# Rows of decays spread to 128 partitions by DMAs of the GpSimd queue instead of products with one-hot columns

## The chip, the core and the metric

The kernel runs on one core of one Trainium2 chip. The core has five instruction streams that run beside each other and meet only at semaphores: TensorE (PE, the matrix engine), VectorE (DVE), ScalarE (ACT), GpSimd (POOL) and SyncE (SP). Each takes its instructions strictly in order, so one that waits holds up all behind it on its engine. Data come in by DMAs, which SP and POOL issue here. The metric is the device time of one execution in microseconds (us), as the median of several runs.

## What is computed

A trunk of two layers over one sequence of 512 tokens, 1024 features, in float32. Each layer is

```
x += 1/2 SwiGLU(RMSNorm(x))
x += W_out concat[mLSTM | retention | gated DeltaNet](RMSNorm(x))
x += 1/2 SwiGLU(RMSNorm(x))
```

and a last RMSNorm follows. The change is in the middle step, the mixer. Two of its three parts weigh pairs of tokens by decays that come from a running quantity per head and token:

```
# gated DeltaNet, per head, per chunk
g = cumsum(log_alpha);  decay[i, j] = exp(g[i] - g[j])   where j <= i
a_mat = I + strict(kb k^T * decay);  sol = triangular_solve(a_mat, rhs)
qk = (q k^T) * decay;  o = (q * exp(g)) S + qk u
# mLSTM, per head, per chunk
w[i, j] = exp(bcum[i] - bcum[j] + i_pre[j] - m_row[i])   where j <= i
```

Both need, for every head, a row of 512 numbers (g, or a running maximum) that varies along the free dimension and is the same on all 128 partitions, while the other index of the pair lies on the partitions. There are 8 such rows in a layer: 4 for the heads of mLSTM, 4 for those of DeltaNet.

## The kernel before, in words

Activations lie with features on the partitions and the 512 tokens along the free dimension. A float32 product is made of three fast products: each weight tile and each activation is split in a high part (`wh`, `xh`) and a low part (`wl`, `xl`), and `mm3` adds wh*xh, wh*xl and wl*xh in one bank of PSUM. The feed-forward steps save some of these products by a scheme of sums (tiles `px`, `py`, `pz`); `pd` are their down projections.

The mixer (`mixer`, from line 793) computes 32 tiles of the input projection (`pin` with features on the partitions, `ptok` with tokens there), 24 fast products each, and 8 tiles of the output projection (`po`). Between these dense products PE gets the small ones of the three recurrences. Each recurrence is written as generators (`gate_math`, `decays`, `delta_inverse`, `q_post`, `chain`, `mlstm`, `retention` and others), which sit in 12 lanes. A planner (`Clock`, `poll`) keeps a guessed time for each engine while the program is recorded and decides after every three dense products which generators may record a step; `wait` holds a generator until a named mark is set. The order that comes out is then fixed in the program: at run time each engine goes through it and waits where a semaphore isn't there yet.

A weight tile of the mixer takes two DMAs of 512 KB. SP loads the raw tile (`wr`). For the low part ACT writes the negated rounded tile to `wl` (line 309), and POOL then issues a DMA that adds the same weights onto it from memory (line 310, `wl<-win`); ACT and DVE write `wh`. `weights` starts the split two tiles ahead. All POOL DMAs go through one queue, named q0 in the profile; those of SP are q1.

The rows of decays: `gate_math` transposes the running sums to 8 rows of 512 (`prow`, line 948), copies them to SBUF and makes the running maximum of the four mLSTM rows by a scan (lines 950 and 951). ACT writes the rounded rows to partitions 0 to 7 of `RB`, DVE the remainder to partitions 32 to 39, and the mark `rows` is set (lines 953 to 957). `SEL` holds one-hot columns, with ones at j and 32 + j. `bcast_row` (line 863) multiplies column j, repeated 128 times, with `RB`: one product of 128x512 on PE, whose result is row j on every partition of a PSUM bank. It is called in three places:

- `decays` (line 1049): four banks `pG`, from which DVE makes `X`, and ACT the exponentials in place; `delta_inverse` multiplies `L` with these.
- `mlstm` (line 1362), once for each of two pairs of heads: two banks `pM`, from which DVE makes the halves of `w1` and other things.
- `q_post`, once for each of four heads: a bank `pG`, from which DVE makes `PT` and ACT the factor `eG` (in a tile `m` or `cs`).

That is 12 products in a layer, 24 in all.

Of the kernel before, what the change touches and what calls it, by code (L numbers as in the profile page):

```python
# [9 lines left out]
F32 = mybir.dt.float32  # L10
F32R = mybir.dt.float32r
I32 = mybir.dt.int32
AF = mybir.ActivationFunctionType
ALU = mybir.AluOpType
AX = mybir.AxisListType

P = 128
S = 512
# [8 lines left out]
INV = 4  # L27
BACKLOG = 1.65
VFIRST = 0.3
WARM = 11  # L30
OUT_KEYS = [("s0",), ("s1",), ("s2",), ("s3",)] + 4 * [("s4", "s5", "s6", "s7")]
GATES = (0, 1, 4, 5, 6, 7, 2, 3)
# [15 lines left out]
    merge_pairs="V c V V c V".split(),  # L48
    mlstm="V A V A V A G V V Vc Vc".split(),
    norm_cols="V A".split(),  # L50
    q_post="A VA A VG".split(),
    retention="VG Vc c".split(),
    rope="VG cG VG cG VG cG VG c".split(),
    split_weights="A c c".split(),
# [7 lines left out]
O_GQ, O_GK, O_GV, O_GZ, O_GA = 2056, 2568, 3080, 3592, 4104  # L62


C_ID, C_TRI, C_ONE, C_MT, C_MS, C_M32, C_COS, C_SIN, C_HALF, C_SEL, C_DEC, C_QD, C_KD, C_GC, C_SUM, C_END = (
    0, 128, 256, 260, 388, 516, 580, 708, 836, 838, 846, 1358, 1614, 1618, 1620, 1636)


Q_N1, Q_NM, Q_N2, Q_MG, Q_RG, Q_GG, Q_CONV, Q_BIAS, Q_ALOG = 0, 8, 16, 24, 26, 28, 32, 80, 96
# [3 lines left out]
def const_table():  # L73
    c = np.zeros((P, C_END), np.float32)
    r = np.arange(P)
    c[:, C_ID:C_ID + P] = np.eye(P)
    c[:, C_TRI:C_TRI + P] = r[:, None] <= r[None, :]
    c[:, C_ONE] = 1.0
    c[:, C_MT:C_MT + P] = np.where(r[:, None] <= r[None, :], 0.0, NEG)
    c[:, C_MS:C_MS + P] = np.where(r[:, None] > r[None, :], 0.0, NEG)  # L80
    c[:, C_M32:C_M32 + 32] = r[:, None] // 32 % 2 == 0
    inv = np.float32(10000.0) ** (-np.arange(0, 64, 2, dtype=np.float32) / np.float32(64))
    ang = (np.arange(S, dtype=np.float32)[:, None] * inv[None, :].astype(np.float32)).astype(np.float64)
    for col, f in ((C_COS, np.cos), (C_SIN, np.sin)):
        c[:, col:col + P] = f(ang).astype(np.float32).reshape(NT, P, 32).transpose(1, 0, 2).reshape(P, P)
    c[:, C_HALF] = r % 2 == 0
    c[:, C_HALF + 1] = r % 2 == 1
    for j in range(8):
        c[j, C_SEL + j] = c[32 + j, C_SEL + j] = 1.0

    lg = np.log1p(-np.exp2(-5.0 - np.arange(4)))
    rel = r[None, :] - r[:, None]
    for j, g in enumerate(lg):
        c[:, C_DEC + j * P:C_DEC + (j + 1) * P] = np.where(rel >= 0, np.exp(np.maximum(rel, 0) * g) * 0.125, 0.0)
        half = slice(64 * (j % 2), 64 * (j % 2) + 64)
        c[half, C_QD + (j // 2) * P:C_QD + (j // 2 + 1) * P] = np.exp((r + 1.0) * g)
        c[:, C_KD + j] = np.exp((P - 1.0 - r) * g) * 0.125
        c[half, C_GC + j // 2] = np.exp(P * g)
    c[:, C_SUM:C_SUM + 16] = r[:, None] % 32 == np.arange(16)[None, :]
    return c  # L100
# [67 lines left out]
def trunk(ctx, tc, a, out):  # L168
# [21 lines left out]
    T, V, A, G = Engine(nc.tensor, "T"), Engine(nc.vector, "V"), Engine(nc.scalar, "A"), Engine(nc.gpsimd, "G")  # L190

    cst = ctx.enter_context(tc.tile_pool(name="cst", bufs=1))
# [33 lines left out]
    def SM(s):  # L226
        if clk[0] is not None:
            clk[0].bank()
        return psm.tile([P, S], F32, name=nm(s), tag="sm")

    def r(ap):
        return ap.bitcast(F32R)
# [11 lines left out]
    def v3(ap, b):  # L244
        return ap.rearrange("p (a b) -> p a b", b=b)

    def bc(ap2, n):
        return ap2.unsqueeze(2).broadcast_to([ap2.shape[0], ap2.shape[1], n])


    C = cst.tile([P, C_END], F32, name="C")
# [3 lines left out]
    maskT = C[:, C_MT:C_MT + P]  # L255
    maskS = C[:, C_MS:C_MS + P]
    half = [C[:, C_HALF + i:C_HALF + i + 1] for i in (0, 1)]

    def bc4(m):
        return m.unsqueeze(1).broadcast_to([P, 4, P])  # L260
# [6 lines left out]

    h = cst.tile([P, KT, S], F32, name="h")
    Z4 = cst.tile([4, 1], F32, name="Z4")
    SEL = cst.tile([P, 8], F32, name="SEL")  # L270
    RB = cst.tile([P, S], F32, name="RB")
    zero = cst.tile([P, 1], F32, name="zero")


    plan, ends = [], deque()
# [492 lines left out]
    def mixer(l, n, nxt, after):  # L768
        q = prm[l]
        ck_ = clk[0] = Clock()  # L770
        marks = ck_.marks

        kdec, gl = COL("kdec", 16), COL("gl", 16)
# [6 lines left out]
        tm = [TMP("m", 520) for _ in range(8)]  # L780
# [79 lines left out]
        def wait(*keys):  # L860
            yield keys

        def bcast_row(ps, j):
            m = ps.shape[0]
            T.matmul(ps, r(SEL[:, j:j + 1].broadcast_to([P, m])), r(RB), start=True, stop=True)

        def norm_cols():
            n.stats()
# [5 lines left out]
        def gate_math():  # L874
# [71 lines left out]
            prow = SM("prow")  # L946
            for t in range(NT):
                T.transpose(prow[0:8, t * P:(t + 1) * P], ag3[:, t, :], ident)
            row = tm[6][0:8, 0:S]
            V.tensor_copy(row, prow[0:8, :])  # L950
            V.tensor_tensor_scan(row[0:4, :], Z4.broadcast_to([4, S]), prow[0:4, :], 0.0, ALU.add, ALU.max)
            yield
            A.copy(r(RB[0:8, :]), row)
            yield
            V.tensor_sub(r(RB[32:40, :]), row, RB[0:8, :])
            env.update(bg3=bg3, ag3=ag3, ng3=ng3, bt=bt)
            mark("rows")
            yield
# [88 lines left out]
        L, X, Tm = U("L"), U("X"), U("Tm")  # L1047

        def decays():

            yield from wait("rows")
            bg3 = env["bg3"]
            for hd in range(4):
                pG = SM("pG")
                bcast_row(pG, 4 + hd)
                E = X[:, hd, :]
                V.tensor_tensor(v3(E, P), bc4(maskS), v3(pG, P), ALU.subtract)
                V.tensor_copy(gl[:, hd * 4:hd * 4 + 4], v3(pG, P)[:, :, P - 1])
                yield
                for t in range(NT):  # L1060
                    s = slice(t * P, (t + 1) * P)
                    A.activation(E[:, s], E[:, s], AF.Exp, bias=bg3[:, t, 4 + hd:5 + hd])
                if hd == 3:
                    mark("decays")
                yield
            bght = bg3[:, :, 4:8].rearrange("p t h -> p h t")
            V.tensor_tensor(v3(kdec, 4), v3(gl, 4), bght, ALU.subtract)
            yield
            A.activation(kdec, kdec, AF.Exp)
            A.activation(eglast, gl, AF.Exp)  # L1070
            eg = COL("eg", 16)
            A.activation(v3(eg, 4), bght, AF.Exp)
            env["eg"] = eg
            mark("eg")
            yield
# [132 lines left out]
        def q_post(hd, kT, qT, odd):  # L1208
            yield from wait(f"q{hd}", "Um")
            if "PT" not in env:  # L1210
                env["PT"] = U("PT")
            PT = env["PT"]
            eG = scratch()[:, 2, :] if odd else tm[7][:, 0:S]
            bg3, ng3 = env["bg3"], env["ng3"]
            ps = to_tok(qT[:, hd, :])
            A.activation(PT[:, hd, :], ps, AF.Square)
            yield
            V.tensor_reduce(ssq[:, hd * 4:hd * 4 + 4], v3(PT[:, hd, :], P), AX.X, ALU.add)
            pG = SM("pG")
            bcast_row(pG, 4 + hd)  # L1220
            V.tensor_tensor(v3(PT[:, hd, :], P), v3(pG, P), bc4(maskT), ALU.add)
            A.activation(eG, pG, AF.Exp)
            yield
            for t in range(NT):
                s = slice(t * P, (t + 1) * P)
                A.activation(PT[:, hd, s], PT[:, hd, s], AF.Exp, bias=ng3[:, t, hd:hd + 1])
            yield
            pp = SM("pP")
            for t in range(NT):
                s = slice(t * P, (t + 1) * P)  # L1230
                T.matmul(pp[:, s], kT[:, hd, s], qT[:, hd, s], start=True, stop=True)
            V.tensor_tensor(PT[:, hd, :], pp, PT[:, hd, :], ALU.mult)
            G.tensor_tensor(qT[:, hd, :], qT[:, hd, :], eG, ALU.mult)
            mark(f"pq{hd}")
            yield
# [127 lines left out]
        def mlstm(pair, mqk, V1):  # L1363
            yield from wait("rows", "mqk", "vv")
            ag3 = env["ag3"]
            h0 = 2 * pair
            Es = [w1[:, 0:S], w1[:, S:2 * S]]
            kw, qs = w2[:, 0:384], w2[:, 384:768]
            mc, mp = COL("mc", 8), COL("mp", 4)
            for b in range(2):  # L1370
                pM = SM("pM")
                bcast_row(pM, h0 + b)
                V.tensor_tensor(v3(Es[b], P), bc4(maskT), v3(pM, P), ALU.subtract)
                hb = slice(64 * b, 64 * b + 64)
                V.tensor_copy(mc[:, 4 * b:4 * b + 4], v3(pM, P)[:, :, P - 1])
                V.tensor_copy(mp[hb, :], mc[hb, 4 * b:4 * b + 4])
                V.tensor_tensor(v3(qs[hb, :], P), bc(mp[hb, 0:3], P), v3(pM[hb, :], P)[:, 1:4, :], ALU.subtract)
                yield
                for t in range(NT):
                    c = slice(t * P, (t + 1) * P)  # L1380
                    A.activation(Es[b][:, c], Es[b][:, c], AF.Exp, bias=ag3[:, t, h0 + b:h0 + b + 1])
                yield
# [336 lines left out]
        T.matmul(warm, idle[:, 0:P], idle, start=True, stop=True)  # L1719
    n = Blocks(prm[0][:, Q_N1:Q_N1 + 8])  # L1720
    G.memset(Z4, 0.0)
    G.memset(zero, 0.0)
    sqs = {}

    def summed(d):
# [19 lines left out]
    summed(7)  # L1745
    gu.load_a(2)
    n.todo += [step for p in range(4) for step in n.sums(p)]
    n.todo.append(lambda: (A.copy(r(SEL), C[:, C_SEL:C_SEL + 8]), A.copy(r(RB), zero.broadcast_to([P, S]))))
    for l in range(DEPTH):
        nm_ = Norm(prm[l][:, Q_NM:Q_NM + 8])  # L1750
        ffn(n, stages[l][0], nm_)
# [73 lines left out]
```

## Time and profile before

| | |
|---|---|
| median of three runs | 2028.41 us (2026.38 to 2029.28) |
| the profiled execution's own time | 2026.25 us |
| its span, first to last instruction | 2024.5 us |
| PE busy | 1992.9 us, 98% |
| DVE busy | 1412.9 us, 70% |
| ACT busy | 1077.3 us, 53% |
| POOL busy | 268.9 us, 13% |
| granted TensorE clock, mean | 0.996 |
| moved by DMAs | 270.18 MB, 133 GB/s |

The profile is one execution. Busy time is what an engine spent in its instructions; matmuls overlap each other, so the time that one adds is read from the distance of two starts, not from its own length. The granted clock is a share of TensorE's upper level (1.00 is 2.4 GHz, 0.50 is 1.2 GHz). In the span the mixer of the first layer lies at about 365 to 620 us, that of the second at about 1360 to 1615.

### The profile page before, as it was taken

To read this page: it belongs to the slowest core of one execution; us is meant where nothing else is said; L and a number is where in the kernel's file an instruction comes from. 1 tells how busy PE (TensorE), PEld (TensorE's weight loads), DVE (VectorE), ACT (ScalarE), POOL (GpSimd) and SP (SyncE) were. 2 spreads that over 40 slices of the span, in tenths; PEclk is the share of its full clock that TensorE was granted. 3 is DMA by queue.
4 is the path that set the end of the run, shared out by engine and by line. 5 is a ranking of instruction groups with operands and counts; after the bars stand their busy time and mean duration, and the time that the engine had idled before them with its cause. 6 is when DMAs were issued, how large, how long until landed. Compare 5 with 4: busy or idle time off the path is not lost.

```text
span 2024.5 us, 32377 instructions
## 1 busy us (share of the span) xinstructions
PE 1992.9 (98%) x12865; PEld 1765.9 (87%) x12865; DVE 1412.9 (70%) x2447; ACT 1077.3 (53%) x1607; POOL 268.9 (13%) x311
## 2 busy tenths in 40 slices
PE   9999999999999999999999999999999999999997
PEld 6999988787888899998889998877878889999886
DVE  6888934568676788883588887335777758888623
ACT  5666622564476566662365555227545756655521
POOL 0000001134212100000010000013132120000000
PEclk9999999999999999999999999999999999999999
DMA  5555422664457466633256663237734655565231
GB/s 191 156 158 161 110 96 91 174 167 105 97 116 187 122 162 162 164 99 108 94 142 158 159 160 109 86 101 176 168 84 104 150 148 151 157 157 157 90 109 50
DMA packets 77928, 270.18 MB, mean 133 GB/s; under 512 B 8912, under 2 KB 11216, under 8 KB 77776
## 3 DMA queue, kind: packets, MB, share of 16 engines
q1 hardware_dynamic: 54080, 184.73, 25.6%
q0 software_dynamic: 22608, 82.32, 24.3%
q8 instruction: 101, 1.65, 0.3%
q10 hardware_dynamic: 1088, 1.05, 0.1%
q14 instruction: 51, 0.42, 0.1%
HBM read 265.97 MB, written 2.10 MB: 132 GB/s over the span
## 4 chain that ended last, share of the span: by engine, by line
PE 90%; DVE 5%; issue 2%; DMA 1%; ACT 1%; SPq 0%; POOL 0%; DVEq 0%; ACTq 0%; POOLq 0%
PE pd L182 22%; PE px L182 16%; PE pin L182 12%; PE pz L182 11%; PE py L182 11%; PE ptok L182 3%; PE pu L182 3%; PE pg L182 2%; DVE X L182 1%; PE pav L182 1%; DVE wl L182 1%; DMA wl<-win 1%; PE po L182 1%; PE ptr L182 1%; DMA m<-wgt 1%
## 5 line engine op out<-in xcount | busy, mean ns | idle before, releaser
L182 PE MATMUL pd<-hid,wh 128*128 128x512 f32 (+1 forms) x1320 | 403.9, 388 | 1.1 <-ACT wh L182 1.1
L182 ACT CAST wh<-wr 128x512 fp32r<-128x512 f32 (+2 forms) x392 | 308.3, 809 | 11.7 <-DMA wr<-w1gu 5.4
L182 DVE TENSOR_TENSOR wl<-wr,wh 128x1024 fp32r<-128x1024 f32 (+2 forms) x276 | 279.1, 1048 | 42.5 <-ACT wh L182 42.2
L182 PEld LDWEIGHTS pd<-hid,wh 128*128 128x128 f32 x1320 | 246.3, 189 | 55.2 <-ACT wh L182 1.3
L182 PE MATMUL pd<-hid,wl 128*128 128x512 f32 (+1 forms) x660 | 255.8, 388 | 0.8 <-DVE wl L182 0.8
L182 PE MATMUL px<-ub,wh 128*128 128x256 f32 x1264 | 232.6, 282 | 1.4 <-DVE g L182 1.4
L182 PE MATMUL py<-ub,wh 128*128 128x256 f32 x1264 | 229.2, 282 | 2.3 <-ACT wh L182 2.3
L182 ACT ACTIVATE g<-g 128x512 f32<-128x512 f32 x96 | 60.5, 632 | 283.7 <-DVE g L182 283.7
L182 DVE TENSOR_TENSOR wl<-s,wh 128x1024 fp32r<-128x1024 f32 x158 | 193.1, 1222 | 12.6 <-ACT wh L182 9.9
L182 PEld LDWEIGHTS py<-ub,wh 128*128 128x128 f32 x1264 | 194.3, 189 | 2.7 <-ACT wh L182 2.7
L182 PEld LDWEIGHTS px<-ub,wh 128*128 128x128 f32 x1264 | 193.8, 188 | 2.5 <-DVE g L182 2.2
L182 PE MATMUL py<-ub,wl 128*128 128x256 f32 x632 | 177.8, 281 | 1.5 <-DVE wl L182 1.5
L182 PE MATMUL pz<-xl,wh 128*128 128x256 f32 x632 | 178.1, 282 | 0.0
L182 ACT ACTIVATE xh<-h,prm 128x512 fp32r<-128x512 f32 x48 | 34.6, 722 | 269.4 <-DVE h L182 268.9
L182 PE MATMUL pz<-xh,wh 128*128 128x256 f32 x632 | 177.6, 281 | 0.0
L182 PE MATMUL px<-ub,wl 128*128 128x256 f32 x632 | 177.5, 281 | 0.0
L182 DVE SCALAR_TENSOR_TENSOR d<-pd,rb 128x512 f32<-128x512 f32 (+1 forms) x33 | 22.3, 675 | 222.3 <-PE pd L182 222.3
L182 PE MATMUL pz<-xh,wl 128*128 128x256 f32 x632 | 177.2, 280 | 0.0
L182 ACT CAST wh<-s 128x1024 fp32r<-128x1024 f32 x158 | 164.7, 1042 | 0.0
L182 PE MATMUL pin<-xh,wh 128*128 128x512 f32 x384 | 161.2, 420 | 0.0
L182 PE MATMUL pin<-xh,wl 128*128 128x512 f32 x384 | 151.3, 394 | 2.5 <-DMA wl<-win 2.5
L182 PE MATMUL pin<-xl,wh 128*128 128x512 f32 x384 | 151.2, 394 | 0.0
(602 smaller groups left out, 4363.4 us busy)
## 6 DMA issues: line engine op xcount, KB each, us to landing
wr<-w2gu SPq DMA_DIRECT2D x88, 512.0 KB, 5.7
wr<-w1gu SPq DMA_DIRECT2D x86, 512.0 KB, 5.6
wr<-win SPq DMA_DIRECT2D x64, 512.0 KB, 4.9
wl<-win POOLq DMA_DIRECT2D x62, 512.0 KB, 6.5
s<-w2gu POOLq DMA_DIRECT2D x40, 512.0 KB, 5.7
s<-w1gu POOLq DMA_DIRECT2D x39, 512.0 KB, 5.7
wr<-w1d SPq DMA_DIRECT2D x32, 512.0 KB, 4.4
wr<-w2d SPq DMA_DIRECT2D x32, 512.0 KB, 4.3
```

Source lines behind the costliest of these rows:

```text
L182: i = f(*a_, **k_)
```

## The change

`RB`, `SEL` and the products with them go, and so do the two steps in `gate_math` that filled `RB`. The 8 rows stay in a tile `ROWS` of 8 partitions. A new function issues a DMA of the POOL queue that reads one row of `ROWS` 128 times and writes it to the 128 partitions of an SBUF tile (256 KB written), and tells the planner that the row is there 3.0 us after its own time:

```diff
+LAND = 3.0
-        def bcast_row(ps, j):
-            m = ps.shape[0]
-            T.matmul(ps, r(SEL[:, j:j + 1].broadcast_to([P, m])), r(RB), start=True, stop=True)
+        def spread(dst, j, key):
+
+            G.dma_start(out=dst, in_=ROWS[j:j + 1, :].unsqueeze(1).broadcast_to([1, P, S]))
+            marks[key] = ck_.t + LAND
...
-            row = tm[6][0:8, 0:S]
+            row = ROWS
             V.tensor_copy(row, prow[0:8, :])
             V.tensor_tensor_scan(row[0:4, :], Z4.broadcast_to([4, S]), prow[0:4, :], 0.0, ALU.add, ALU.max)
-            yield
-            A.copy(r(RB[0:8, :]), row)
-            yield
-            V.tensor_sub(r(RB[32:40, :]), row, RB[0:8, :])
             env.update(bg3=bg3, ag3=ag3, ng3=ng3, bt=bt)
             mark("rows")
...
             for hd in range(4):
-                pG = SM("pG")
-                bcast_row(pG, 4 + hd)
+                spread(X[:, hd, :], 4 + hd, f"g{hd}")
+            for hd in range(4):
+                yield from wait(f"g{hd}")
                 E = X[:, hd, :]
-                V.tensor_tensor(v3(E, P), bc4(maskS), v3(pG, P), ALU.subtract)
-                V.tensor_copy(gl[:, hd * 4:hd * 4 + 4], v3(pG, P)[:, :, P - 1])
+                V.tensor_copy(gl[:, hd * 4:hd * 4 + 4], v3(E, P)[:, :, P - 1])
+                V.tensor_tensor(v3(E, P), bc4(maskS), v3(E, P), ALU.subtract)
...
-            pG = SM("pG")
-            bcast_row(pG, 4 + hd)
-            V.tensor_tensor(v3(PT[:, hd, :], P), v3(pG, P), bc4(maskT), ALU.add)
-            A.activation(eG, pG, AF.Exp)
+            spread(PT[:, hd, :], 4 + hd, f"G{hd}")
+            yield from wait(f"G{hd}")
+            A.activation(eG, PT[:, hd, :], AF.Exp)
+            V.tensor_tensor(v3(PT[:, hd, :], P), v3(PT[:, hd, :], P), bc4(maskT), ALU.add)
...
             for b in range(2):
-                pM = SM("pM")
-                bcast_row(pM, h0 + b)
-                V.tensor_tensor(v3(Es[b], P), bc4(maskT), v3(pM, P), ALU.subtract)
+                spread(Es[b], h0 + b, f"M{h0 + b}")
+            for b in range(2):
+                yield from wait(f"M{h0 + b}")
+                pM = Es[b]
...
+                V.tensor_tensor(v3(Es[b], P), bc4(maskT), v3(pM, P), ALU.subtract)
```

The planner lays out the mixer anew around this. Three places matter below. The first is POOL's queue at the first decays of layer 1 (`wl` are low parts of weight tiles, `Tm` is a scratch tile of `delta_inverse`). Before:

```order
46 L182 DMA wl_3860<-win 128x1024
47 L182 DMA wl_3901<-win 128x1024
48 L182 DMA wl_3962<-win 128x1024
49 L182 TENSOR_TENSOR Tm_3588<-L_3586,C 128x512 x2
50 L182 DMA wl_4035<-win 128x1024
```

The same place in the changed kernel:

```order
45 L181 DMA wl_3855<-win 128x1024
46 L181 DMA X_3582<-ROWS 128x1x512 x4
47 L181 DMA wl_3908<-win 128x1024
48 L181 TENSOR_TENSOR Tm_3583<-L_3581,C 128x512 x2
49 L181 DMA wl_3964<-win 128x1024
```

The four spreads stand together, ahead of the low part of the weight tile that was next in the queue before. The second place is DVE at the same decays (`kT` a convolution, `mqk` an evacuated dense tile, `gl` the last column of each block). Before:

```order
398 L182 TENSOR_TENSOR RB<-m_3582,RB 8x512
399 L182 TENSOR_TENSOR mqk_3856<-pin_3863,rb_3666 128x512
400 L182 TENSOR_TENSOR flo_3922<-pmc_3917,bg_3812 128x16
401 L182 TENSOR_TENSOR X_3587<-C,pG_3924 128x512
402 L182 COPY gl_3563<-pG_3924 128x4
403 L182 TENSOR_TENSOR X_3587<-C,pG_3951 128x512
```

And in the changed kernel:

```order
398 L181 SCALAR_TENSOR_TENSOR kT_3584<-m_3574,prm_86,kT_3584 128x512 x3
399 L181 COPY gl_3558<-X_3582 128x4
400 L181 TENSOR_TENSOR X_3582<-C,X_3582 128x512
401 L181 TENSOR_TENSOR mqk_3851<-pin_3858,rb_3661 128x512
402 L181 CAST wh_3907<-wr_3852 128x512
403 L181 COPY L_3581<-pL_3938 128x512
```

The copy of `gl` is now the first reader of the spread row, and the evacuation of a dense tile, half a split of a weight tile and the evacuation of a product `pL` are queued behind it. The third place is POOL at the first pair of `mlstm` (`X` is here the scratch of the inverse, `w_515` the tile `w1`). Before:

```order
57 L182 DMA wl_4227<-win 128x1024
58 L182 MEMSET X_3587 128x512
59 L182 COPY X_3587<-C 128x16 x2
60 L182 DMA wl_4292<-win 128x1024
61 L182 DMA wl_4335<-win 128x1024
```

And in the changed kernel:

```order
57 L181 DMA wl_4230<-win 128x1024
58 L181 MEMSET X_3582 128x512
59 L181 COPY X_3582<-C 128x16 x2
60 L181 DMA w_515_3579<-ROWS 128x1x512 x2
61 L181 DMA wl_4296<-win 128x1024
62 L181 DMA wl_4342<-win 128x1024
```

Before, the copies to `X` were followed by the weight tile at once; two spreads now stand between them.

## Rows read from the trace of the kernel before

**Rows 1.** The page: busy time, share of the span, instructions of each engine
```profile
PE 1992.9 (98%) x12865; PEld 1765.9 (87%) x12865; DVE 1412.9 (70%) x2447; ACT 1077.3 (53%) x1607; POOL 268.9 (13%) x311
```
**Rows 2.** The page: chain of work that ended last, by engine
```profile
PE 90%; DVE 5%; issue 2%; DMA 1%; ACT 1%; SPq 0%; POOL 0%; DVEq 0%; ACTq 0%; POOLq 0%
```
**Rows 3.** Busy time by stretch: us, engines, clock, DMA share, GB/s
```profile
365.00:600.00 235.00, 229.64 (x1461) 187.21 (x1461) 166.56 (x420) 142.35 (x249) 67.40 (x85) 1.00 0.58 133
1360.00:1620.00 260.00, 255.05 (x1585) 207.86 (x1584) 185.10 (x474) 158.25 (x274) 70.83 (x89) 1.00 0.59 135
```
**Rows 4.** Instructions on pG and pM: ns min/median/max, first and last start
```profile
L182 PE MATMUL pG<-RB,SEL x16: 389/476/500, 399.2 to 1576.9; 128*128 128x512 f32 x16
L182 PE MATMUL pM<-RB,SEL x8: 392/393/482, 442.8 to 1474.0; 128*128 128x512 f32 x8
```
**Rows 5.** PE in order of time: start, us, instruction
```profile
410.11 0.39 PE L182 MATMUL pG<-RB,SEL 128*128 128x512 f32 x1
410.34 0.39 PE L182 MATMUL pin<-xh,wh 128*128 128x512 f32 x1
...
411.84 0.48 PE L182 MATMUL pin<-xh,wh 128*128 128x512 f32 x1
412.16 0.40 PE L182 MATMUL pin<-xl,wh 128*128 128x512 f32 x1
412.40 0.39 PE L182 MATMUL pin<-xh,wl 128*128 128x512 f32 x1
...
452.63 0.40 PE L182 MATMUL ptok<-wl,xh 128*128 128x512 f32 x1
```
**Rows 6.** The page: queues: packets, MB, share of 16 engines
```profile
q1 hardware_dynamic: 54080, 184.73, 25.6%
q0 software_dynamic: 22608, 82.32, 24.3%
```
**Rows 7.** DMA issues: engine, count, KB, us to landing
```profile
out<-h SPq DMA_DIRECT2D x4, 256.0 KB, 2.4
```
**Rows 8.** DMA queues and issues in 385 to 455 us
```profile
q0 software_dynamic: 1564, 5.69, 45.4%
...
wl<-win POOLq DMA_DIRECT2D x11, 512.0 KB, 7.0
```
**Rows 9.** PE alone by stretch: PE busy, clock, DMA share, GB/s
```profile
10.00:15.00 5.00, 4.39 (x11) 0.56 1.05 413
```
**Rows 10.** DVE in order of time, idle before in brackets
```profile
392.05 1.21 DVE L182 TENSOR_TENSOR_SCAN m<-Z,prow 4x512 f32<-4x512 f32 x1
...
399.72 0.69 DVE L182 TENSOR_TENSOR X<-C,pG 128x512 f32<-128x512 f32 x1 [0.26 <-PE pG L182]
```
**Rows 11.** POOL in order of time, idle before in brackets
```profile
391.02 0.86 POOL L182 DMA_DIRECT2D wl<-win  x1 [7.20 <-ACT wl L182]
395.91 0.86 POOL L182 DMA_DIRECT2D wl<-win  x1 [4.03 <-ACT wl L182]
...
435.45 0.88 POOL L182 DMA_DIRECT2D wl<-win  x1 [9.31 <-ACT wl L182]
...
443.18 0.87 POOL L182 DMA_DIRECT2D wl<-win  x1 [5.92 <-ACT wl L182]
```
**Rows 12.** PE's waits in 365 to 600 us: total, times, longest
```profile
PE pin L182 <- DMA wl<-win: 1.5, 1, 1.5
PE ptr L182 <- ACT vb L182: 1.0, 1, 1.0
...
PE psc L182 <- DVE Tm L182: 0.4, 1, 0.4
```
**Rows 13.** ACT in order of time, second place where PE serves q_post
```profile
549.48 0.60 ACT L182 ACTIVATE m<-pG 128x512 f32<-128x512 f32 x1 [2.35 <-DVE PT L182]
```

More of the change, by code (lines that the diff above doesn't have):

```diff
@@ L50 @@
     norm_cols="V A".split(),
-    q_post="A VA A VG".split(),
+    q_post="A V VA A VG".split(),
     retention="VG Vc c".split(),
@@ L62 @@
 O_GQ, O_GK, O_GV, O_GZ, O_GA = 2056, 2568, 3080, 3592, 4104
-C_ID, C_TRI, C_ONE, C_MT, C_MS, C_M32, C_COS, C_SIN, C_HALF, C_SEL, C_DEC, C_QD, C_KD, C_GC, C_SUM, C_END = (
-    0, 128, 256, 260, 388, 516, 580, 708, 836, 838, 846, 1358, 1614, 1618, 1620, 1636)
+C_ID, C_TRI, C_ONE, C_MT, C_MS, C_M32, C_COS, C_SIN, C_HALF, C_DEC, C_QD, C_KD, C_GC, C_SUM, C_END = (
+    0, 128, 256, 260, 388, 516, 580, 708, 836, 846, 1358, 1614, 1618, 1620, 1636)
 Q_N1, Q_NM, Q_N2, Q_MG, Q_RG, Q_GG, Q_CONV, Q_BIAS, Q_ALOG = 0, 8, 16, 24, 26, 28, 32, 80, 96
@@ L87, in const_table @@
     c[:, C_HALF + 1] = r % 2 == 1
-    for j in range(8):
-        c[j, C_SEL + j] = c[32 + j, C_SEL + j] = 1.0
     lg = np.log1p(-np.exp2(-5.0 - np.arange(4)))
@@ L269, in trunk @@
     Z4 = cst.tile([4, 1], F32, name="Z4")
-    SEL = cst.tile([P, 8], F32, name="SEL")
-    RB = cst.tile([P, S], F32, name="RB")
-    zero = cst.tile([P, 1], F32, name="zero")
+    ROWS = cst.tile([8, S], F32, name="ROWS")
     plan, ends = [], deque()
@@ L1721, in trunk @@
     G.memset(Z4, 0.0)
-    G.memset(zero, 0.0)
     sqs = {}
@@ L1747, in trunk @@
     n.todo += [step for p in range(4) for step in n.sums(p)]
-    n.todo.append(lambda: (A.copy(r(SEL), C[:, C_SEL:C_SEL + 8]), A.copy(r(RB), zero.broadcast_to([P, S]))))
     for l in range(DEPTH):
```

## Prediction, written before the result was known

> **What bounds the kernel now.** I read the page's busy times first: PE is busy 1992.9 of 2024.5 us, the next engine, DVE, 70% [rows 1]. The chain that ended last is 90% PE [rows 2], so PE's own work and PE's waits are the time, and anything else counts only through a wait of PE. Then the two mixers by stretch: PE 229.64 of 235 us and 255.05 of 260, at the upper clock throughout, with the DMA engines busy 0.58 and 0.59 of the time [rows 3]. The reader is to see there that PE loses only about 5 us in each mixer, and that the DMA engines are more than half taken by weights. Last I read the order of time on PE, DVE and POOL around the places of the change [rows 5, 10, 11], to see what stands behind what.
>
> **What goes.** 16 products pG and 8 pM [rows 4]. Each holds PE for the distance to the next start: 410.11 to 410.34, so 0.23 us [rows 5]. Where that distance is larger it is the step between kinds of products, which the dense product pays anyway (411.84 to 412.16 with no pG beside it) [rows 5]. 24 x 0.23 = 5.5 us, all on the path since PE has no gaps: -5.5 us. The cast and the subtraction that filled RB, and the set-up of RB and SEL, ran on ACT and DVE, 53% and 70% busy [rows 1], beside dense products: nothing. The readers on DVE and ACT read SBUF instead of PSUM, one instruction for one (0.69 us for X) [rows 10]: nothing, as long as DVE has its slack of 30%.
>
> **What comes: issue.** 24 DMAs on POOL at 0.86 us, the length of POOL's present ones [rows 11]: 20.6 us on an engine that is busy 13% [rows 1]. They delay the weight tile behind them by at most 4 x 0.86 = 3.4 us. The tile issued at 395.91 is first used at 412.40 [rows 5, 11] and lands in 7.0 [rows 8], so 9.5 us are free: nothing.
>
> **What comes: how long a spread takes.** No row shows a DMA that reads one partition. The bounds: below, the same 256 KB out of SBUF, all 128 partitions on both sides and nothing beside it, lands in 2.4 us [rows 7]. Above, the 128 reads of a spread all go to one row in one partition; if they can't be shared out they go one after another at the rate of one engine. The fastest stretch that I found is 413 GB/s over 16 engines, 25.8 GB/s each [rows 9]: 262144 B / 25.8 = 10.2 us. By the mean of q1, 184.73 MB in 25.6% of 16 x 2024.5 us, it is 22.3 GB/s and 11.8 us [rows 6]. What makes 2.4 us possible is that both sides lie in 128 partitions; here one side doesn't, so the row of one engine's rate is nearer, and I take 10.2.
>
> On this two pages of the Trainium skill speak against each other. "DMA: Bandwidth & Descriptors", Anatomy of one DMA, gives about 2.0 us plus bytes over 436 GB/s for a POOL DMA, an estimate of 2.6 us here: within the planner's 3.0, and a small gain. "SBUF — State Buffer", Door 1, says that the rate depends on how many of 16 ports the partitions reach, and measures 27.6 GB/s on four partitions of one port: an estimate of 9.5 us here. The weight tiles' 7.0 us [rows 8] is longer than the first rule, at 512 KB, would say (3.2 by estimate). No run here has the one-partition case.
>
> **What it costs: the four of decays.** The rows are ready when the scan ends, 392.05 + 1.21 = 393.3 [rows 10]. The weight tile ahead in the queue was issued at 391.02 and has landed by 398.0 [rows 8, 11]. POOL's DMAs share one queue, so I take them to be served in order: the four spreads are through at 398.0 + 4 x 10.2 = 438.8. The low part behind them then needs its own share, 45.4% of 70 us over 11 tiles = 2.9 us [rows 8], and some 1.7 us to be reported (the 2.4 us of [rows 7] less 0.7 us, which 256 KB take on 16 engines at 22.3 GB/s each [rows 6]), together 4.6: 443.4. PE needs it at 412.40 less the four products gone, 411.5 [rows 5]. PE waits 32 us. DVE waits over the same time, as its copy of gl is the first reader of each spread, with the evacuations behind it; it is done at about 440, so this adds nothing to PE's wait.
>
> **The first pair of mlstm.** The two spreads follow the tile issued at 435.45, landed at 442.5 [rows 8, 11]: 442.5 + 20.4 + 4.6 = 467.5 for the tile behind, which PE uses at 452.63 [rows 5] less two products: 452.2. PE waits 15 us.
>
> **The second pair.** Weight tiles come less often here, so the queue has room, but DVE is the partner of PE in the small products of the inverse: PE already waits for it and for ACT by 0.4 and 1.0 us [rows 12], so nothing stands between. The planner expects the row after 3.0 us. The two spreads hold DVE 10.2 - 3.0 = 7 and then 10 us; PE has about one dense tile of other work, 24 x 0.23 = 5.5 us. Between 0 (all hidden) and 17; I take 12.
>
> **q_post, four heads.** Each spread now starts after DVE's sum of PT and is read by ACT for eG, an instruction that before waited only 2.35 us [rows 13]. ACT is held 10.2 + 1.7 - 3.0 = 9 us, and behind it stand copies of the chain that PE waits for and casts of weights. 3 of the 9 us are covered by PE's dense products between the steps of the chain (three to nine of them, 0.7 to 2.1 us, and one step). 4 x 6 = 24, between 0 and 36.
>
> **Sum.** 32 + 15 + 12 + 24 = 83 us in a layer, 166 in two, less 5.5: +160.5. Made against the profiled execution's own 2026.25 (span 2024.5 and 1.75 around it), that is 2186.8; the median of the runs is 2.2 us higher, so 2189.
>
> **The rivals.**
>
> First, on the other side: the spreads are shared out over the 16 engines like the 256 KB of [rows 7] and land in 2.4 us, under the 3.0 that the planner put in. Then the queue is held for 0.7 us each, no reader waits, and only the 5.5 us are left: 2026.25 - 5.5 + 2.2 = 2023. For it speaks that row, and that nothing else in the profile forbids it; against it, that it reads 128 partitions and a spread reads one. It decides up to a landing of about 4 us, from where ACT's and DVE's waits eat the gain. The new order of the mixer alone may move it by the 5 us that PE loses in a mixer now [rows 3], so part of this case is no change.
>
> Second: shared out, but landing like the weight tiles of the same queue, 7.0 us among the other traffic [rows 8]. The four of decays and the first pair then fit in the 9.5 us that a tile has. DVE and ACT are held 4 us beyond the plan in the second pair and q_post, six places, half of it covered: 12 a layer, 24 - 5.5 = +18.5: 2047.
>
> Third: spreads so slow that they move at q0's own mean, 82.32 MB in 24.3% of 16 x 2024.5 us = 10.5 GB/s an engine, 25 us each [rows 6]. Decays: 398 + 100 + 4.6 - 411.5 = 91; first pair 442.5 + 50 + 4.6 - 452.2 = 45; second pair and q_post by the same proportion about 130: 266 a layer, 2555. Against it: q0's packets add onto memory that they read first, a spread only copies.
>
> **How the numbers follow.** 0.62 for the forecast, with a range of its own from 2115 (only the waits for weight tiles count: 2 x 47 - 5.5 = +88.5) to 2255 (11.8 us a spread: 38 + 18 + 15 + 32 = 103 a layer, which gives 2229, and some 26 us for a lowered clock after the waits; in [rows 9], where PE has gaps, it was granted 0.56, between its two levels). 0.18 for the first rival, 0.14 for the second, 0.06 for the third. What a measurement of this kernel can tell from no change is 0.2%, 4 us. The first rival is faster in 0.12 and within 4 us in 0.06; with a little of the second next to it, 0.07 for no change, and 0.81 for slower. The range for 8 in 10 leaves out the faster part and the third rival: 2026 to 2255.
>
> **What would show it.** The DMAs from ROWS: landing of 10 us and more, the last of the four of decays some 40 us after its issue; or 2 to 4 us, and then the first rival holds. PE's waits: pin and ptok for wl at the tile after the four spreads, some 30 us once a layer, where the mixer of before has 1.5 us at most [rows 12]. DVE idle before gl, ACT idle before eG. PE's busy time should fall by the 24 products, and the two feed-forward stretches should take as long as before; if they don't, my account of the place is wrong. If the spreads take 10 us and PE still doesn't wait, the queue isn't served in order, and the weight tiles pass them.

## The result, and the profile after

The changed kernel takes 2189.71 us in the median of six runs (2187.67 to 2191.32); the kernel before took 2030.09 beside it (2026.38 to 2032.02). The ratio is 1.0788, 95% interval 1.0774 to 1.0802. The forecast was 2189.

The page of the kernel after, against [rows 1], [rows 2] and [rows 6]: busy times, the chain that ended last, and the two queues (packets, MB, share of 16 engines' span, which is now 2187.9 us).

```profile
PE 2020.6 (92%) x12841; PEld 1784.0 (82%) x12841; DVE 1396.3 (64%) x2431; ACT 1083.2 (50%) x1617; POOL 281.6 (13%) x334
...
q0 software_dynamic: 24528, 88.62, 31.8%
q1 hardware_dynamic: 54080, 184.73, 23.5%
...
PE 78%; DMA 14%; DVE 4%; issue 2%; ACT 2%; POOL 1%; SPq 0%; DVEq 0%; ACTq 0%; POOLq 0%
```

Two things are to be read from the first row. PE issues 24 instructions fewer, as it should, yet is busy 27.7 us longer. And its idle time, span less busy, went from 31.6 to 167.3 us: +135.7. The two sum to the span's +163.4. In the chain, DMAs rose from 1% to 14%.

The waits of PE over the whole span (us in total, times, longest); in the mixer of before the longest wait for a weight tile was 1.5 us [rows 12]:

```profile
PE pin L181 <- DMA wl<-win: 70.3, 6, 26.1
PE ptok L181 <- DMA wl<-win: 32.5, 2, 16.5
PE pt L181 <- DVE Tm L181: 21.3, 4, 8.3
PE pS L181 <- ACT vb L181: 9.4, 2, 4.7
PE ptr L181 <- ACT qT L181: 5.4, 2, 2.8
...
PE prt L181 <- DVE R L181: 2.6, 2, 1.3
```

That is 141.5 us for two layers, and 102.8 of it is for weight tiles, which no edit touched. In order of time in the first layer (start, us, instruction, idle before it), to be laid beside [rows 5]:

```profile
441.34 0.79 PE L181 MATMUL pin<-xh,wl 128*128 128x512 f32 x1 [26.10 <-DMA wl<-win]
...
499.11 0.80 PE L181 MATMUL ptok<-wl,xh 128*128 128x512 f32 x1 [15.93 <-DMA wl<-win]
...
538.76 0.63 PE L181 MATMUL pt<-Tm,m 64*32 64x32 f32 x8 [8.35 <-DVE Tm L181]
...
626.17 2.07 PE L181 MATMUL pS<-vb,cs 128*128 128x128 f32 x8 [4.74 <-ACT vb L181]
...
645.76 1.12 PE L181 MATMUL ptr<-C,qT 128*128 128x128 f32 x4 [2.83 <-ACT qT L181]
...
671.32 0.79 PE L181 MATMUL pin<-xh,wl 128*128 128x512 f32 x1 [7.92 <-DMA wl<-win]
```

The first is the place of decays, the second the first pair of mlstm, the third (with 2.57 and 1.28 us soon after it) the second pair, the last three q_post. DVE's first reader of each spread shows how long one takes:

```profile
408.75 0.17 DVE L181 COPY gl<-X 128x4 f32<-128x4 f32 x1 [8.90 <-DMA X<-ROWS]
...
418.39 0.17 DVE L181 COPY gl<-X 128x4 f32<-128x4 f32 x1 [6.62 <-DMA X<-ROWS]
...
438.33 0.17 DVE L181 COPY gl<-X 128x4 f32<-128x4 f32 x1 [7.39 <-DMA X<-ROWS]
```

From 408.75 to 438.33 there are three spreads, 9.86 us each: 262144 B in that is 26.6 GB/s. What the 16 DMA engines do meanwhile, by stretch (us, the engines in the order PE, PEld, DVE, ACT, POOL, then granted clock, DMA share, GB/s), and by queue in 398 to 438 us:

```profile
408.00:418.00 10.00, 7.24 (x38) 5.78 (x36) 2.99 (x6) 4.50 (x8) 3.51 (x3) 1.00 0.99 28
418.00:428.00 10.00, 0.00 (x0) 0.00 (x0) 2.39 (x5) 1.75 (x5) 1.26 (x1) 0.60 0.93 27
428.00:438.00 10.00, 0.00 (x0) 0.00 (x0) 2.65 (x5) 3.25 (x7) 1.02 (x2) 0.50 0.86 56
```

```profile
q0 software_dynamic: 438, 1.46, 92.5%
q1 hardware_dynamic: 157, 0.58, 3.6%
...
wl<-win POOLq DMA_DIRECT2D x3, 512.0 KB, 32.5
wr<-win SPq DMA_DIRECT2D x3, 512.0 KB, 27.7
```

All 16 engines count as busy, and they move 27 GB/s together. A raw tile of SP, on the other queue, takes 27.7 us to land as well. In [rows 3] the engines moved 133 GB/s at a share of 0.58.

Last, PE alone as it comes out of the 26 us wait (us, PE busy, granted clock, DMA share, GB/s):

```profile
436.00:441.00 5.00, 0.00 (x0) 0.50 0.91 220
441.00:446.00 5.00, 4.66 (x11) 0.50 1.05 275
446.00:451.00 5.00, 5.00 (x20) 0.86 1.00 265
451.00:456.00 5.00, 5.00 (x24) 1.00 0.90 206
```

While PE stood idle the clock fell to the lower of its two levels (0.50, 1.2 GHz). PE restarts there: 11 products in 4.66 us, where it does 24 in 5 us at 2.4 GHz. This is where the longer busy time comes from.

### The profile page after: what moved, and what is told of

It reads as the page before. It is cut to its first block, busy times and chain, and to the rows that moved or that the text cites. A ratio compares the mean times of both kernels' runs of the same rounds, so it can differ in the third digit from the quotient of the medians.

```text
span 2187.9 us, 32370 instructions
## 1 busy us (share of the span) xinstructions
PE 2020.6 (92%) x12841; PEld 1784.0 (82%) x12841; DVE 1396.3 (64%) x2431; ACT 1083.2 (50%) x1617; POOL 281.6 (13%) x334
## 3 DMA queue, kind: packets, MB, share of 16 engines
q0 software_dynamic: 24528, 88.62, 31.8%
q10 hardware_dynamic: 1088, 1.05, 0.1%
## 4 chain that ended last, share of the span: by engine, by line
PE 78%; DMA 14%; DVE 4%; issue 2%; ACT 2%; POOL 1%; SPq 0%; DVEq 0%; ACTq 0%; POOLq 0%
PE pd L181 20%; PE px L181 15%; PE pz L181 10%; PE py L181 10%; DMA wl<-win 9%; PE pin L181 7%; PE ptok L181 3%; PE pu L181 2%; DMA PT<-ROWS 2%; PE pg L181 2%; DMA w<-ROWS 2%; PE pav L181 1%; DVE wl L181 1%; PE po L181 1%; ACT wh L181 1%
## 5 line engine op out<-in xcount | busy, mean ns | idle before, releaser
L181 PE MATMUL pin<-xh,wl 128*128 128x512 f32 x384 | 159.4, 415 | 70.3 <-DMA wl<-win 70.3
L181 PE MATMUL pin<-xh,wh 128*128 128x512 f32 x384 | 171.3, 446 | 0.0
L181 PE MATMUL pin<-xl,wh 128*128 128x512 f32 x384 | 158.5, 413 | 0.0
```

Source lines behind the costliest of these rows:

```text
L181: i = f(*a_, **k_)
```

## The experiments

My theory: a spread is held to some 26.6 GB/s because it reads one partition of SBUF; each place then costs PE its own wait, for a weight tile that is kept from landing or for a reader on DVE or ACT; and each long wait costs more through the clock. Rivals: the cost is the order of POOL's one queue, the count of reads, the broadcast of one row as such, or the planner's number for the landing (3.0 us). "Over" is against the runs of the kernel before in the same set, whose medians lie between 2027.4 and 2029.1 us.

| run | over, us | ratio, 95% interval | PE idle | clock |
|---|---|---|---|---|
| source on 128 partitions | 11.7 | 1.0045 to 1.0078 | 43.1 | 0.990 |
| spreads on ACT's queue | 156.3 | 1.0752 to 1.0784 | 154.5 | 0.959 |
| half of each row | 90.2 | 1.0430 to 1.0461 | 101.1 | 0.975 |
| rows in HBM | 29.6 | 1.0113 to 1.0167 | 48.1 | 0.989 |
| four adjacent partitions | 205.7 | 1.0991 to 1.1027 | 209.4 | 0.950 |
| four partitions, 4 apart | 33.1 | 1.0147 to 1.0181 | 52.6 | 0.985 |
| decays alone | 60.2 | 1.0282 to 1.0312 | 86.6 | 0.981 |
| mlstm alone | 55.7 | 1.0265 to 1.0297 | 79.8 | 0.976 |
| q_post alone | 42.6 | 1.0200 to 1.0228 | 64.9 | 0.985 |
| planner told 11 us and more | 234.9 | 1.1124 to 1.1196 | 222.2 | 0.940 |
| rows in HBM, planned at 3.0 us | 11.5 | 1.0040 to 1.0070 | 42.3 | 0.990 |
| HBM without mlstm | 19.9 | 1.0082 to 1.0116 | 45.6 | 0.989 |

### Source on 128 partitions

The same bytes, the same queue, the same order, but each partition reads its own data.

```diff
-            G.dma_start(out=dst, in_=ROWS[j:j + 1, :].unsqueeze(1).broadcast_to([1, P, S]))
+            G.dma_start(out=dst, in_=ROWS)
```

> The 24 DMAs stay where they are in the GpSimd queue, with the same 256 KB each, but read 128 partitions (each its own) in place of one row 128 times. What is left out: the rows reach only the first 8 partitions, the others get zeros, and the log decays are scaled by 0.01 so that numbers stay finite. Theory of the one row (reads of one partition are served at one port's or one engine's rate): landing falls from 10 us apiece to 3 to 7 us, PE's waits for wl go, the clock stays up, and the time is 2020 to 2032 us. Rival, that any 256 KB from SBUF to SBUF on this queue takes that long: landing stays at 10 us a piece, the time at 2190 us.

Landing (KB, median us) and the tile behind the spreads:

```profile
X<-ROWS POOLq DMA_DIRECT2D x8, 256.0 KB, 5.1
```

```profile
PE pin L181 <- DMA wl<-win: 2.2, 2, 1.1
```

The landing fell from 27.3 to 5.1 us in decays, the waits for weight tiles went, and with them 148 us. So the loss is in how the source lies, and neither in 24 DMAs more on POOL nor in the bytes. The time is 9 us above the top of what I expected: something besides the transfer costs 12 us, which is taken up at the end.

### Spreads on ACT's queue

```diff
-            G.dma_start(out=dst, in_=ROWS[j:j + 1, :].unsqueeze(1).broadcast_to([1, P, S]))
+            A.dma_start(out=dst, in_=ROWS[j:j + 1, :].unsqueeze(1).broadcast_to([1, P, S]))
```

> The 24 spreads are issued from ScalarE's queue, so the weight tiles of the GpSimd queue are no longer behind them. If only the order in the queue costs: wl lands in about 7 us, PE's waits for wl (103 us) go, the waits for DVE and ACT (36 us) and some clock stay: about 2085 us. If the reads of one row hold all 16 DMA engines, whatever queue they stand in: each spread still takes 10 us, wl crawls beside it, PE still waits 10 to 30 us at the tile after the four spreads, and the time is 2130 to 2200 us.

2185.38 us: the same. With the spreads on q10, POOL's queue was nearly empty in 398 to 438 us, and still its weight tiles and SP's landed late:

```profile
q10 hardware_dynamic: 536, 0.97, 78.4%
q0 software_dynamic: 147, 0.58, 7.3%
...
wl<-win POOLq DMA_DIRECT2D x3, 512.0 KB, 19.2
wr<-win SPq DMA_DIRECT2D x3, 512.0 KB, 20.2
```

A place in the queue is thus not what a tile needs; the engines are held for all queues. One thing muddies this place: the four issues held ACT itself for 20.85 us, so POOL's next tile was issued late too.

```profile
392.99 20.85 ACTq L181 DMA_DIRECT2D X<-ROWS  x4
```

So the equal time is in part chance: over the whole span PE waited 75.4 us for weight tiles, where it had waited 102.8, and 20.3 us for ACT before `pL` were new. The first pair of mlstm is free of this. ACT issued its two spreads in 1.1 us, POOL issued the next tile at 471.39, with its queue free of spreads, and PE still waited 15.57 us for that tile, against 15.93 with all in one queue:

```profile
495.62 0.79 PE L181 MATMUL ptok<-wl,xh 128*128 128x512 f32 x1 [15.57 <-DMA wl<-win]
```

### Half of each row

256 of 512 columns are spread.

```diff
-            G.dma_start(out=dst, in_=ROWS[j:j + 1, :].unsqueeze(1).broadcast_to([1, P, S]))
+            G.memset(dst[:, 256:512], 0.0)
+            G.dma_start(out=dst[:, 0:256], in_=ROWS[j:j + 1, 0:256].unsqueeze(1).broadcast_to([1, P, 256]))
```

> Each spread moves 256 of the 512 columns: still 128 reads of one row, each of 1 KB instead of 2 KB. What is left out: the second half of each row is set to zero by a memset on POOL (0.3 us), and the log decays are scaled by 0.01. If bytes set the time: 4.9 us a spread, PE's waits a layer fall from 70 to about 20 us, the time is about 2070 us. If each read has a fixed price (128 x 77 ns): 9.9 us a spread still, 2190 us.

DVE's readers stood at 398.96, 403.70, 408.46 and 413.60 us, 4.9 apart where the whole rows were 9.9. The program names 128 reads in both kernels, but the queue's packets fell too, from 80 to 48 a spread (q0 has 22608 in the kernel before, 24528 in the changed one, 23760 here), so this run alone doesn't part bytes from pieces. The run on ACT's queue does: a spread took 144 packets there (q10's 4544 less the 1088 of before), and by q10's share (9.3% of 16 spans, before 0.1%) it took 134 engine-us (one of the 16 engines busy for 1 us), against 136 by the growth of q0's share in the changed kernel. So bytes set the time, at the same 27 GB/s. Of the time itself my forecast missed: 2119.33, not about 2070. Waits of PE on the output tiles (`po`, for `yr` and `yh`, some 19 us) came in, and some 30 us of lowered clock (PE is busy 2017.1 us, against 1992.9 less 5.5); I had foreseen neither.

### Rows in HBM

The eight rows are stored to HBM once in a layer, and the 24 spreads read them there; the planner is told 5 us, in decays 7.

```diff
+            A.dma_start(out=HROWS, in_=ROWS)
...
-            G.dma_start(out=dst, in_=ROWS[j:j + 1, :].unsqueeze(1).broadcast_to([1, P, S]))
+            G.dma_start(out=dst, in_=HROWS[j:j + 1, :].unsqueeze(1).broadcast_to([1, P, S]))
```

> The eight rows are first stored to a row buffer in HBM by one 16 KB DMA of ACT's queue, twice in the kernel, and the 24 spreads read HBM rows; the planner is told 5 us for a landing, 7 us for the four of decays. Theory (128 reads of one partition of SBUF go through one port and hold all 16 engines): HBM has no such partition, so a spread lands in 3 to 7 us, the queue is free, PE's waits for the weight tiles go, q0's share falls back to 25%, and the time is 2018 to 2040. Rival (the cause is that all 128 reads fetch one and the same row, wherever it lies): a spread still takes 8 us or more, the waits for weight tiles stay, and the time is 2110 or more.

```profile
X<-HROWS POOLq DMA_DIRECT2D x8, 256.0 KB, 9.5
...
PT<-HROWS POOLq DMA_DIRECT2D x8, 256.0 KB, 5.2
```

One row read 128 times is quick if it lies in HBM (four in a row have landed after 9.5 us, with the store ahead of them), and 130 us come back. So it isn't the broadcast as such. The 2058.50 is above the range, and its six runs lie from 2047.62 to 2067.14, wider than any other kernel here but the one told 11 us and more; why stays open.

### Four adjacent partitions, and four that are 4 apart

Each spread reads four partitions, 32 times each.

```diff
-            G.dma_start(out=dst, in_=ROWS[j:j + 1, :].unsqueeze(1).broadcast_to([1, P, S]))
+            G.dma_start(out=dst, in_=ROWS[0:4, :].unsqueeze(1).broadcast_to([4, 32, S]))
```

and `ROWS[0:16:4, :]` in the other kernel.

> The changed kernel, each spread reading the four adjacent partitions 0 to 3, 32 times each, instead of one partition 128 times; left out: the right row (four rows of the tile are spread instead), and the logarithms of the decays are scaled by 0.01 so that the numbers stay finite. Theory A (one port serves a group of partitions, of which 0 to 3 are one, by the Trainium skill, SBUF - State Buffer, Door 1): still some 10 us a spread, the weight-tile waits of the changed kernel stay, 2170 to 2195. Theory B (what is slow is that one partition is read over and over): four partitions, a quarter of the time, 2.5 us a spread, and 2035 to 2060.

> As the run with four adjacent partitions, with the four source partitions 0, 4, 8 and 12. Theory A (a port for each group of four): four ports, 2.5 us a spread, waits for weight tiles gone, 2035 to 2060. Theory B (one partition is slow by itself): the same 2.5 us as with adjacent ones. If both runs take 10 us a spread, neither holds, and it is the broadcast read as such.

Adjacent: 2233.64 us. Apart: 2061.10. The same bytes in the same count of DMAs from the same number of partitions, and only which partitions differs. Adjacent first: the landing, DVE's first reader, and a stretch in which the four spreads run; then landing and stretch of the kernel with partitions 0, 4, 8 and 12.

```profile
X<-ROWS POOLq DMA_DIRECT2D x8, 256.0 KB, 43.2
```

```profile
438.76 0.17 DVE L181 COPY gl<-X 128x4 f32<-128x4 f32 x1 [40.30 <-DMA X<-ROWS]
```

```profile
418.00:428.00 10.00, 0.00 (x0) 0.00 (x0) 0.00 (x0) 0.00 (x0) 0.00 (x0) 0.50 0.95 25
```

```profile
X<-ROWS POOLq DMA_DIRECT2D x8, 256.0 KB, 12.9
```

```profile
408.00:418.00 10.00, 10.00 (x53) 8.53 (x52) 7.65 (x12) 6.25 (x13) 4.79 (x4) 1.00 0.83 161
```

Four adjacent partitions are as slow as one (DVE gets the first of the four spreads at 438.76 and waits for none after it; the changed kernel gets its fourth at 438.33). Four that lie 4 apart are 3.3 times as fast. So the limit belongs to a group of partitions. The Trainium skill has this rule ("SBUF — State Buffer", Door 1): a DMA's rate depends on how many of 16 ports its partitions reach, with 0 to 3 on one port and 0, 4, 8, 12 on four. It gives 27.6 GB/s for a port, and the trace 26.6 GB/s; that it also binds a DMA that reads the same bytes over and over is what these two runs show.

The adjacent kernel is 44 us slower than the changed one, which my range didn't hold. The four spreads landed together (43.2 us is the median of all eight), so DVE had nothing at all for 40 us, where in the changed kernel it got a row every 10 us. Why they came together here and one by one there stays open.

### The three places one by one

The place named keeps its spreads, read from the rounded rows in `RB`; the two others make products as before, as here q_post:

```diff
-            spread(PT[:, hd, :], 4 + hd, f"G{hd}")
-            yield from wait(f"G{hd}")
-            A.activation(eG, PT[:, hd, :], AF.Exp)
-            V.tensor_tensor(v3(PT[:, hd, :], P), v3(PT[:, hd, :], P), bc4(maskT), ALU.add)
+            pG = SM("pG")
+            bcast_row(pG, 4 + hd)
+            V.tensor_tensor(v3(PT[:, hd, :], P), v3(pG, P), bc4(maskT), ALU.add)
+            A.activation(eG, pG, AF.Exp)
```

> Only decays reads spread rows (8 of the 24 DMAs, from the rounded rows in RB, so the remainder is left out); mlstm and q_post keep their products. By my sum: one wait of 26 us a layer, some 6 us of lowered clock after it, 8 products less (-1.8 us): 2028 + 62 = 2090 us. Rival, that the waits of a mixer stand in for one another and the last one sets the end: either hardly any change (below 2050 us) or nearly all of it (above 2150 us).

> Only the eight spreads of mlstm are kept, of the changed kernel; decays and q_post use products again. Theory (each place costs its own wait, and they add): first pair 15.9 us of waiting for the weight tile, second pair 12.2 us through DVE, both in each layer, some 10 us of lowered clock, less 8 products of 0.23: 2029 + 56 + 10 - 2 = 2093. Rival (the places cost so much only because the four spreads of decays push all later transfers back): the first pair finds its tile landed, and the time is 2060 or less.

> Only the eight spreads of q_post are kept, four in a layer, each read by ACT at once. Theory (waits add): 15.5 us a layer, a few us of lowered clock, less 8 products: 2029 + 31 + 5 - 2 = 2063. With decays alone (60 us over) and mlstm alone (64 expected) the three make 158, against 161 for the whole change. Rival (my own term of 24 us a layer): 2029 + 48 - 2 = 2075 before any clock loss.

Measured 2089.34, 2084.61 and 2071.48: decays as I expected, mlstm 8 us less, q_post 8 us more. They lie over the kernel before by 60.2, 55.7 and 42.6, together 158.5, where the whole change is 159.6 over. The parts add, so each place pays for itself, and the first pair of mlstm waits for its tile (12.5 us in the first layer) without the spreads of decays before it. Decays hit its time, but not by the wait that I had: PE waited 20.4 us for its tile, not 26, and 4.3 us for DVE before that. PE's main waits, of mlstm alone and then of q_post alone:

```profile
PE prt L183 <- DVE R L183: 27.8, 2, 14.3
PE ptok L183 <- DMA wl<-win: 25.9, 2, 13.3
```

```profile
PE pin L183 <- DMA wl<-win: 18.2, 4, 8.0
PE pS L183 <- ACT vb L183: 9.7, 2, 4.8
PE ptr L183 <- ACT qT L183: 6.5, 2, 4.0
```

q_post alone stays under the rival: its waits (34.4 us in two layers) are near those of q_post in the whole change (31), but PE's busy time is 14.6 us above that of before less 8 products (2005.7 against 1992.9 - 1.8), a clock loss of three times my guess.

### The planner told the truth

```diff
-LAND = 3.0
+LAND = 11.0
...
-            marks[key] = ck_.t + LAND
+            marks[key] = ck_.t + LAND + 10.0 * k
```

with k the number of spreads issued just before it in decays and mlstm, and 0 in q_post.

> The changed kernel with the planner told what a spread takes: 11 us, and 10 us more for each further one issued beside it, instead of 3.0. Theory (the loss in decays and in the first pair of mlstm is the weight tile queued behind the spreads, which a due time doesn't move; the rest is ACT and DVE held by a row that comes late, which it does): the waits for weight tiles stay at 26 and 16 us a layer, those for DVE and ACT shrink, the time is 2130 to 2160. Rival (all the loss is the planner's wrong number): PE finds other work everywhere, 2060 or less.

2263.78 us, 74 more than the changed kernel: both expectations fell. The waits for weight tiles stayed (115.3 us, in the changed kernel 102.8), as the theory said, since a due time frees no engine. But those for DVE didn't shrink. PE's waits, and the busy times in a stretch of the first layer:

```profile
PE pin L181 <- DMA wl<-win: 87.8, 9, 26.5
PE ptr L181 <- DVE Tm L181: 41.2, 2, 20.6
PE ptok L181 <- DMA wl<-win: 27.5, 2, 13.9
```

```profile
520.00:560.00 40.00, 17.18 (x84) 13.50 (x83) 38.26 (x75) 15.50 (x27) 11.50 (x16) 0.73 0.34 79
```

The rows that the planner now held back met other work of DVE: there DVE is busy 38.26 of 40 us, PE 17.18, and PE's longest wait, 20.6 us, is for the `Tm` that DVE makes. A truer number gave a worse order.

### What is left when the transfer is cheap

The kernel with the rows in HBM, planned with 3.0 us again, and the same with mlstm's rows made by products:

```diff
-LAND = 5.0
+LAND = 3.0
...
-                spread(X[:, hd, :], 4 + hd, f"g{hd}", 7.0)
+                spread(X[:, hd, :], 4 + hd, f"g{hd}")
```

> The kernel with the row buffer in HBM, planned with 3.0 us for each landing as in the changed kernel, instead of 5 and 7. If the 29 us that it stands over the kernel before come from landings later than planned, they grow: 2060 to 2080. If they come from the order that a longer due time gives, it goes to the time of the run with the wide source, 2035 to 2045.

> The spreads of decays and of q_post read the row buffer in HBM, mlstm makes its rows by products as before (16 products of 0.23 us fewer). If what the kernel with all spreads from HBM stands over the one before (11 us) comes from the second pair of mlstm, where PE waited 4 us a layer for ACT and the granted clock fell to 0.66 in one stretch of 10 us, this kernel is 2022 to 2027, faster than both by up to 4 us. If it comes from the order of decays and q_post, it is 2035 to 2042.

2039.49 and 2047.29 us. The first is what the order theory said, and equals the run with 128 source partitions (1.0055 and 1.0062 times before): with this order, two quite different cheap transfers end 12 us above the kernel before. In its profile PE is idle 10.7 us more than before, and busy 3.7 more, although 24 products (5.5 us) are gone, so some 9 us are lowered clock. Of those 10.7 us, 8.1 are one wait, 4 us a layer, with a lowered clock behind it (first row and stretch below, of the first kernel). In my expectation I took it for the second pair of mlstm. That was wrong: POOL issues the spreads of the second pair only at 485.71, and DVE waits for none of the first pair's. PE waits there for what ACT makes, and ACT has just waited for the `X` of DVE's triangular inverse (third row). So it is the order and not a landing. With 128 source partitions 8.8 us of PE's idle time are the same wait. The last run has another order again and doesn't have this wait, but the time rose, above both ranges: PE waits elsewhere, as in q_post (last row).

```profile
472.55 1.08 PE L181 MATMUL ptr<-C,Tm 128*128 128x128 f32 x4 [4.07 <-ACT rx L181]
```

```profile
470.00:480.00 10.00, 7.45 (x42) 6.24 (x43) 6.96 (x12) 5.90 (x10) 3.73 (x5) 0.66 0.40 81
```

```profile
470.45 1.28 ACT L181 COPY Tm<-X 32x512 f32<-32x512 f32 x2 [3.13 <-DVE X L181]
```

```profile
600.51 0.80 PE L183 MATMUL po<-vb,PT 128*128 128x128 f32 x2 [3.61 <-DVE PT L183]
```

No version here beats the kernel before. The idle part of the 12 us is thus mostly this wait; which step of the planner's new order brings it, and whether an order without such waits can be had, is not settled.

## Why the prediction was right, by its steps

The time was forecast to 1 us, but this closeness is partly luck: two errors cancel, waits 27 us too long and a clock that I had left out of the sum.

| term, us in a layer | forecast | measured |
|---|---|---|
| decays | 32 | 26.1 |
| first pair of mlstm | 15 | 15.9 |
| second pair | 12 | 12.2 |
| q_post | 24 | 15.5 |
| all four, two layers | 166 | 139.4 |
| lowered clock, two layers | 0 | 33.2 |
| products gone | -5.5 | -5.5 (taken over) |
| small waits of before that went | 0 | about -4 |
| sum | 160.5 | 163.4 |

- **A spread, 10.2 us**: 9.9. The size was right, and so was what I chose between 2.4 [rows 7] and 11.8: what makes it slow is that the source lies in one place. My reason was half right. I said that the reads go one after another at the rate of one engine [rows 9]. But q0's share times 16 spans rose from 7871 to 11132 engine-us, 136 for each of 24 spreads: 8.5 us on all 16 engines, not 10 on one. So all engines are taken, and what they wait for is, by the runs with four partitions, one group of partitions, whose rate happens to be near that of an engine. I also misread [rows 7]: `out` lies in HBM, so its 2.4 us is not a transfer inside SBUF, and ACT's queue stored the other half of it beside. Inside SBUF, out of 128 partitions, the same bytes landed in 2.3 to 5.6 us.
- **The queue is served in order**: true, and not what decides. SP's raw tiles took 27.7 us beside the spreads, and with the spreads on ACT's queue PE waited 15.57 us at the first pair instead of 15.93. The sign of error that I had named, weight tiles that pass the spreads, doesn't come even with a queue of their own.
- **Decays, 32**: the four spreads were through 3.2 us sooner than by my sum (the tile ahead in the queue took less than its full 7.0 us out of their time, and each spread 0.3 less), the tile behind them needed 3.0 instead of 4.6, and PE asked for it 1.0 later; the program before this place had moved by 2.75 us (POOL's issue at 391.02 [rows 11] now at 393.77). 32 - 3.2 - 1.6 - 1.0 = 26.2.
- **First pair, 15**, by the same sum: 15.9, and 12.5 with mlstm alone.
- **Second pair, 12**, an estimate between 0 and 17: 8.35 + 2.57 + 1.28 = 12.2, through DVE, as forecast.
- **q_post, 24**: 15.5, the mis-sized step. I let each of four heads expose 6 us through ACT. Two of them did, 4.74 and 2.83 us. Half of the loss, 7.92, is one that I didn't have there at all, again for a weight tile: the spreads of the last two heads are issued at 645.87 and 648.54, and the tile right behind them, at 649.09. While PE waits for it, a wait for ACT at these two heads can't show.
- **The clock, 0**: I had it in the range alone, at 26 us. PE's busy time is 2020.6 against 1992.9 less 5.5, so 33.2 us. Summed over the traces, PE is busy for 77.2 us at the lower level, before for 9.8, and half of the difference, 33.7 us, agrees. It should have stood in the sum: my own steps forecast idle stretches of 12 to 32 us on PE, and the trace of before already showed at its start, where PE has gaps, a lowered clock [rows 9].
- **The products, -5.5**, and POOL's issues at nothing (0.55 us each, four in 2.18): no run measures the products by themselves; the 33.7 us of the clock leave -6.0 for them.
- **The signs.** PE's busy time didn't fall by the 24 products but rose, which I had named as a sign against my account of the place; the clock explains it. The other sign held: from the last `po` of the first mixer to the first `pin` of the second PE took 692 us before and 692 us after.
- **The rivals.** The 128 source partitions gave nearly the first rival's condition, a spread that isn't held by one place, with landings of 2.3 to 5.6 us (I let it decide up to about 4). Even so it was 2040.86, not 2023: it lay near my second rival, 2047, though not by its mechanism, since the order of the mixer costs 12 us, more than the 5 us that I allowed it.

## What to carry to other kernels

Price a DMA by both of its sides, and the narrower one by how many groups of partitions it touches, not by its bytes alone. A transfer that is slow for such a reason is paid for by every other transfer, whichever queue it stands in, so look for the price at the next tile that the bottleneck engine needs. And where a forecast has the matrix engine wait as here, 8 to 26 us at a time, add the lowered clock after it as a term of its own: here about a quarter on top of the waits, and with q_post alone, whose waits are shorter, 14.6 us on 34.4.

## What was not expected of the hardware

- A 256 KB read of one partition, or of four adjacent ones, held all 16 DMA engines some 95% busy at 25 to 28 GB/s.
- Four such DMAs issued by ACT held ACT for 20.85 us, two for 1.1 us; POOL issued its four in 2.18 us.
- From HBM, 128 reads of one 2 KB row aren't slow: a spread alone landed in a median of 3.6 us in q_post (planned at 3.0 us).

```profile
PT<-HROWS POOLq DMA_DIRECT2D x8, 256.0 KB, 3.6
```
